# HGRN level scores in two batches of four levels, with the far half as a step of its own

## The chip, the cores and the metric

The kernel runs on one core of a Trainium2 chip. Its time is the device time of one execution in microseconds (us), the median over several runs. A core has five engines that run side by side, each through its own list of instructions in order: TensorE (PE, matrix products; PEld are its weight loads), VectorE (DVE), ScalarE (ACT), GpSimd (POOL) and SyncE (SP). They wait for one another through semaphores. SP and POOL issue the transfers (DMA) between DRAM and the on-chip memory.

## The reference, cut to what matters

One transformer-like layer over 256 latent tokens and 256 context tokens, width 2048, all in float32. The part around the change is the token mixer's gated linear recurrence (HGRN2) in both directions, with 8 heads of 128 channels:

```python
def step(s, xs):
    qc, kc, vc, gc = xs
    a = jnp.cumsum(gc, axis=2)
    inter = jnp.einsum('bhtk,bhkv->bhtv', qc * jnp.exp(a), s)
    diff = a[:, :, :, None, :] - a[:, :, None, :, :]
    decay = jnp.exp(jnp.where(tri[:, :, None], diff, -jnp.inf))
    scores = jnp.einsum('bhtk,bhsk,bhtsk->bhts', qc, kc, decay)
    intra = jnp.einsum('bhts,bhsv->bhtv', scores, vc)
    s_new = exp(a_last) * s + einsum('bhsk,bhsv->bhkv', kc * exp(a_last - a), vc)
    return s_new, inter + intra

def hgrn_bidir(q, v, gf, gb, s0f, s0b):
    o_f, s_f = hgrn_chunk_scan(q, gf[1], v, gf[0], s0f)
    o_b, s_b = hgrn_chunk_scan(fl(q), fl(gb[1]), fl(v), fl(gb[0]), s0b)
    return o_f + fl(o_b), s_f, s_b
```

Each output token reads each earlier token (in the other direction each later one) with a score that is a product over channels of query, key and all forget gates between the two. The remaining layer is large matrix products: an input projection of 2048 x 11264, two branch projections, an output projection, and an MLP of 2048 x 8192 and back.

## The kernel before, in words

TensorE's large products use a split form: each float32 weight tile of 128 x 1024 is loaded as `raw`, copied by ScalarE to its high half `whi` (L124), and VectorE makes the low half `wlo` (L127). Four such pairs are kept ready ahead of their use (`AHEAD = 4`). Lines 188, 255 and 257 are the products with them; L188 runs as two matmuls with `whi` and one with `wlo` per 128 rows of weights. Between the tiles stand products of vectors with the modulation weights on VectorE (L1314).

The heads are generators (`head`, L1419). While TensorE works through the input projection, `pump` (L161) is called after every few large matmuls and gives some microseconds of credit, and up to three generators emit their next instructions: a positive `yield` uses credit, `yield None` ends the generator's turn until the next call. For the heads, a call comes after 12 L188 matmuls, and later after 8 of L255 and 8 of L257. A scheduler then sets the order on each engine from this; on TensorE it keeps the order in which the program emits, but for one piece. Each engine runs its list as it stands and waits where something is not ready.

A head does this. It holds in `x6` six blocks of 256 columns, with queries and keys of both directions (128 channels by 256 tokens). For a level m, tokens that lie in neighbouring blocks of m score each other; after each level `decay(m)` (L1461) multiplies the gates into one half of each pair of blocks, so the next level can work on blocks twice as wide. The levels are 0 (the token itself), 1, 2, 4, 8, 16, 32, 64 and 128. For levels up to 64, ScalarE gathers the two sides of the product, `left` and `right` (`side`, L1455, the copies are at L1458), four matmuls of 64 output columns by 64 (L1497) write the scores of the 256 tokens into a PSUM bank, and masked copies on VectorE (L1514) put each level's scores into its places of `sc`. The bank holds several levels, and they are multiplied in one batch. The last level of a batch reads its right side straight from `x6` through `halves`, so that its decay must wait until the batch has read it. Level 128, called far, is two matmuls of 128 columns read in place (L1504). Where a batch stands between large products, TensorE goes from weights of 128 columns to two halves of 64 columns and back.

After level 128 the keys are needed with tokens on partitions: VectorE flips 32 x 32 squares (L1523), POOL writes the page to DRAM as `kthere` (L1526) and reads it back in four pieces (L1528), ScalarE copies it as `kt` (L1534), and TensorE builds the states (L1540). ScalarE copies them (L1543), and the head's output is the product of the queries with the states (L1549) and of the scores with the values (L1551). A head waits in its first steps until the head two before it has ended; `x6` has two buffers.

Of the kernel before, what the change touches and what calls it, by code (L numbers as in the profile page):

```python
# [15 lines left out]
P = 128  # L16
T = 256
# [120 lines left out]
class Kernel:  # L138
# [1280 lines left out]
    def head(self, h, e, vp):  # L1419
# [8 lines left out]
        nc = self.nc  # L1428
# [8 lines left out]
        x6 = self.sp.tile([P, 6 * T], F32, name="x6", tag="x6", bufs=2)  # L1437
# [8 lines left out]
        sc = self.small(512, "sc")  # L1446
        sc4 = sc.rearrange("p (c t) -> p c t", c=4)
        near = sc[:, P:2 * P]
        near2 = near.rearrange("p (b t) -> p b t", b=2)

        def halves(o, step, n, m):

            return bass.AP(x6.tensor, x6.offset + o, [x6.ap[0], [2 * m, n // (2 * m)], [step + m, 2], [1, m]])

        def side(name, o, step, m):  # L1455

            t = self.small(T, name)
            nc.scalar.copy(out=t.rearrange("p (n s m) -> p n s m", s=2, m=m), in_=halves(o, step, T, m))  # L1458
            return t

        def decay(m):  # L1461

            lo = x6[:, 0:3 * T].rearrange("p (n w) -> p n w", w=2 * m)[:, :, 0:m]
            hi = x6[:, 3 * T:6 * T].rearrange("p (n w) -> p n w", w=2 * m)[:, :, m:2 * m]
            d = e[:, 0:4 * T].rearrange("p (n w) -> p n w", w=2 * m)
            nb = 3 * T // (2 * m)
            no = T // (2 * m)
            nc.vector.tensor_tensor(lo, lo, d[:, 0:nb, m:m + 1].broadcast_to([P, nb, m]), op=ALU.mult)
            nc.vector.tensor_tensor(hi, hi, d[:, no:no + nb, 0:1].broadcast_to([P, nb, m]), op=ALU.mult)
            if m < 128:  # L1470
                nc.vector.tensor_tensor(d[:, :, 0:1], d[:, :, 0:1], d[:, :, m:m + 1], op=ALU.mult)

        for levels in ((0, 1, 2), (4, 8, 16), (32, 64, 128)):
            ops = []
            for m in levels:
                if m == 0:
                    ops.append((m, ks, q))
                    continue
                if m == 128:
                    yield None  # L1480
                    break
                left = side("left", T, 3 * T, m)
                right = None
                if m != levels[-1]:
                    right = side("right", 2 * T, T, m)
                ops.append((m, left, right))
                yield None
                if right is not None:
                    decay(m)
                    yield 1.2  # L1490
            ps = self.bank()
            for n, (m, left, right) in enumerate(ops):
                for b in range(2):
                    for g in range(2):
                        o = b * P + g * 64
                        r = b * P + (1 - g) * 64 if m == 64 else o
                        nc.tensor.matmul(ps[64 * g:64 * g + 64, n * P + b * 64:n * P + b * 64 + 64], left[:, o:o + 64],  # L1497
                                         right[:, r:r + 64] if right is not None else halves(2 * T + o, T, 64, m), start=True, stop=True)
            if levels[-1] == 128:
                far = self.bank()  # L1500
                for b in range(2):
                    w = x6[:, T:T + P] if b == 0 else x6[:, 4 * T + P:5 * T]
                    r = x6[:, 3 * T + P:4 * T] if b == 0 else x6[:, 2 * T:2 * T + P]
                    nc.tensor.matmul(far[:, b * P:(b + 1) * P], w, r, start=True, stop=True)  # L1504
            for n, (m, _, _) in enumerate(ops):
                pv = ps[:, n * P:(n + 1) * P].rearrange("p (b t) -> p b t", b=2)
                if m == 0:
                    nc.scalar.copy(out=near, in_=ps[:, n * P:(n + 1) * P])
                elif m == 64:
                    for g in range(2):  # L1510
                        nc.scalar.copy(out=sc4[64 * g:64 * g + 64, 0::3, 64 - 64 * g:128 - 64 * g], in_=pv[64 * g:64 * g + 64])
                else:
                    i = LEVELS.index(m)
                    nc.vector.copy_predicated(near2, self.masks[:, i:i + 1, :].broadcast_to([P, 2, 64]), pv)  # L1514
            if levels[-1] == 128:
                for g in range(2):
                    nc.scalar.copy(out=sc4[64 * g:64 * g + 64, 0::3, 64 * g:64 * g + 64], in_=near2[64 * g:64 * g + 64])
                nc.scalar.copy(out=sc4[:, 1:3, :], in_=far[:, :T].rearrange("p (b t) -> p b t", b=2))
            decay(levels[-1])
            yield 1.8  # L1520
        flip, back = e[:, 0:512], e[:, 512:1024]
        for d, o in enumerate((0, 5 * T)):
            nc.vector.transpose(out=flip.rearrange("p (j b r) -> p b j r", j=4, b=4)[:, 2 * d:2 * d + 2],  # L1523
                                in_=x6[:, o:o + T].rearrange("p (b j r) -> p b j r", b=2, j=4))
# [12 lines left out]
        ps = self.bank()  # L1537
# [8 lines left out]
        for tb in range(2):  # L1546
            o = po[:, tb * P:(tb + 1) * P]
# [6 lines left out]
        o = self.at(self.on, h)  # L1554
# [182 lines left out]
```

## Time and profile before

| what | value |
|---|---|
| median of 3 runs | 1623.03 us (1620.81 to 1623.83) |
| the profiled execution | 1622.89 us, span 1620.8 us |
| TensorE busy | 1603.9 us, 99% |
| VectorE busy | 1160.9 us, 72% |
| ScalarE busy | 803.8 us, 50% |
| GpSimd busy | 74.0 us, 5% |
| mean granted TensorE clock | 0.999 |
| moved by DMA | 395.21 MB, 244 GB/s |

The profile is of one execution. The span runs from its first to its last instruction; the time has 2.1 us around it. A row of a timeline has the start in us from the span's start, the length in us, the engine, the line of the kernel, the operation, the tile it writes and those it reads, and in brackets the idle time ahead of it and what ended that. An x behind it counts records; an fp32 matmul with fp32 operands leaves two records. Matmuls overlap, so the time that one costs is read from start to start and not from its length. In a row of grouped instructions the figures behind the bar are busy us, mean ns of one, and the idle time ahead of them.

### The profile page before, as it was taken

The page shows a single profiled execution, that of the slowest core. Times are in us where ns is not written, and L with a number is a line of the kernel's source. Part 1 is how long each engine was busy: PE and PEld are TensorE (multiplying, and loading weights), DVE is VectorE, ACT ScalarE, POOL GpSimd, SP SyncE. Part 2 cuts the span into 40 slices and gives each one's busy share as a digit, 9 for nine tenths or more (in the row PEclk, how much of TensorE's full clock was granted, in tenths as well). Part 3 has the DMA queues.
Part 4 walks back from the last instruction along what each step waited for, and adds up shares of the span by engine and source line. Part 5 has one row for each costly group of instructions (what it writes and reads, how often), then busy time and mean ns, then how long its engine had stood idle before and what let it go on. Part 6 is the DMA issues. An engine that isn't in the chain of part 4 may idle for free.

```text
span 1620.8 us, 22095 instructions
## 1 busy us (share of the span) xinstructions
PE 1603.9 (99%) x8163; PEld 1321.3 (82%) x8163; DVE 1160.9 (72%) x1694; ACT 803.8 (50%) x1166; POOL 74.0 (5%) x138
## 2 busy tenths in 40 slices
PE   7999999999999999999999999999999999999998
PEld 5668888888888888888888888888888888888887
DVE  5786888888778889967887766555665656656556
ACT  6553445465554444653446655444443454435543
POOL 0000001001100000000000001000010011001000
PEclk9999999999999999999999999999999999999999
DMA  9997955554666566778887378866997688777663
GB/s 368 403 391 261 324 200 180 170 162 165 224 228 222 182 195 208 228 265 305 326 289 263 134 262 249 276 207 222 289 288 235 212 264 270 236 241 243 230 218 116
DMA packets 110813, 395.21 MB, mean 244 GB/s; under 512 B 13552, under 2 KB 14448, under 8 KB 110704
## 3 DMA queue, kind: packets, MB, share of 16 engines
q1 hardware_dynamic: 102096, 368.34, 66.4%
q0 software_dynamic: 8320, 25.19, 5.3%
q8 instruction: 64, 1.05, 0.3%
q14 instruction: 45, 0.37, 0.1%
q10 hardware_dynamic: 288, 0.26, 0.0%
HBM read 381.15 MB, written 12.58 MB: 243 GB/s over the span
## 4 chain that ended last, share of the span: by engine, by line
PE 94%; DMA 2%; DVE 2%; ACT 1%; issue 1%; SPq 0%; ACTq 0%; DVEq 0%
PE bank L188 83%; PE bank L255 5%; PE bank L257 2%; PE bank L1497 1%; DMA raw<-wi 1%; DVE wlo L127 1%; DMA x<-x 0%; DMA raw<-wpw 0%; PE bank L1549 0%; PE bank L1551 0%; ACT whi L124 0%; PE bank L1540 0%; DMA fg<-kthere 0%; PE bank L1504 0%; PE bank L1360 0%
## 5 line engine op out<-in xcount | busy, mean ns | idle before, releaser
L127 DVE TENSOR_TENSOR wlo<-raw,whi 128x1024 fp32r<-128x1024 f32 x488 | 593.1, 1223 | 328.5 <-ACT whi L124 324.6
L124 ACT ACTIVATE whi<-raw 128x1024 fp32r<-128x1024 f32 x488 | 512.2, 1058 | 577.2 <-PE bank L188 376.3
L188 PE MATMUL bank<-whi,h 128*128 128x512 f32 x2160 | 674.0, 390 | 2.0 <-DVE h L673 1.2
L188 PEld LDWEIGHTS bank<-whi,h 128*128 128x128 f32 x2160 | 405.2, 188 | 87.6 <-DVE h L673 2.0
L188 PE MATMUL bank<-wlo,h 128*128 128x512 f32 x1080 | 420.8, 390 | 1.4 <-DVE wlo L127 1.4
L188 PEld LDWEIGHTS bank<-wlo,h 128*128 128x128 f32 x1080 | 202.8, 188 | 44.7 <-DVE wlo L127 3.2
L188 PE MATMUL bank<-whi,hidh 128*128 128x512 f32 x503 | 195.0, 388 | 0.0
L188 PE MATMUL bank<-wlo,hidh 128*128 128x512 f32 x503 | 195.0, 388 | 0.0
L188 PE MATMUL bank<-whi,hidl 128*128 128x512 f32 x503 | 195.0, 388 | 0.0
L188 PE MATMUL bank<-h,whi 128*128 128x512 f32 x512 | 163.7, 401 | 0.3 <-DVE h L673 0.3
L188 PEld LDWEIGHTS bank<-h,whi 128*128 128x128 f32 x512 | 92.5, 188 | 23.9 <-issue 5.8
L188 PEld LDWEIGHTS bank<-whi,hidh 128*128 128x128 f32 x503 | 94.5, 188 | 19.5
L188 PEld LDWEIGHTS bank<-wlo,hidh 128*128 128x128 f32 x503 | 94.5, 188 | 19.3
L188 PEld LDWEIGHTS bank<-whi,hidl 128*128 128x128 f32 x503 | 94.5, 188 | 19.2
L188 PE MATMUL bank<-h,wlo 128*128 128x512 f32 x256 | 100.1, 391 | 0.0
L255 PE MATMUL bank<-h,whi 128*128 128x512 f32 x384 | 97.0, 394 | 0.0
L255 PEld LDWEIGHTS bank<-h,whi 128*128 128x128 f32 x384 | 69.1, 189 | 12.7
L1301 DVE SCALAR_TENSOR_TENSOR gacc<-raw,silu_c,gacc 128x1024 f32<-128x1024 f32 x60 | 76.7, 1278 | 0.0
L1314 DVE SCALAR_TENSOR_TENSOR raw<-raw,silu_row 128x1024 f32<-128x1024 f32 x64 | 76.6, 1218 | 0.0
L188 PEld LDWEIGHTS bank<-h,wlo 128*128 128x128 f32 x256 | 48.0, 188 | 10.0
L257 PEld LDWEIGHTS bank<-h,wlo 128*128 128x128 f32 x384 | 52.4, 190 | 3.8
L257 PE MATMUL bank<-h,wlo 128*128 128x256 f32 x384 | 53.5, 282 | 0.0
(252 smaller groups left out, 1377.0 us busy)
## 6 DMA issues: line engine op xcount, KB each, us to landing
raw<-w SPq DMA_DIRECT2D x256, 512.0 KB, 4.8
raw<-wi SPq DMA_DIRECT2D x172, 512.0 KB, 4.4
raw<-wmt SPq DMA_DIRECT2D x64, 512.0 KB, 4.1
raw<-wm SPq DMA_DIRECT2D x64, 512.0 KB, 4.7
rawpage<-wm SPq DMA_DIRECT2D x42, 512.0 KB, 10.0
raw<-wo SPq DMA_DIRECT2D x32, 512.0 KB, 4.6
raw<-who SPq DMA_DIRECT2D x16, 512.0 KB, 4.8
raw<-wpw SPq DMA_DIRECT2D x16, 512.0 KB, 5.5
```

Source lines behind the costliest of these rows:

```text
L124: kn.his.append(nc.scalar.activation(out=hi, in_=raw, func=AF.Copy))
L127: kn.los.append(nc.vector.tensor_tensor(lo, raw, hi.bitcast(F32), op=ALU.subtract))
L188: ins = fn(*args, **kw)
L255: nc.tensor.matmul(bank, w[0][:, cut(i)], x(k)[2], start=(k == 0), stop=False)
L257: nc.tensor.matmul(bank[:, T:], w[1][:, cut(i)], x(k)[0], start=False, stop=(k == nk - 1))
L1301: nc.vector.scalar_tensor_tensor(acc, raw, s, acc, op0=ALU.mult, op1=ALU.add)
L1314: nc.vector.scalar_tensor_tensor(raw, raw, 1.0, self.srow, op0=ALU.mult, op1=ALU.mult, accum_out=self.dot[:, 32 * j + b:32 * j + b + 1])
L1497: nc.tensor.matmul(ps[64 * g:64 * g + 64, n * P + b * 64:n * P + b * 64 + 64], left[:, o:o + 64], right[:, r:r + 64] if right is not None ...
```

## The change

The levels are computed in two batches, (0, 1, 2, 4) and (8, 16, 32, 64), where there were three, (0, 1, 2), (4, 8, 16) and (32, 64, 128). Level 64's two sides are read in place from `x6`; before, ScalarE gathered them. The first gathered right side of a batch is put into the second half of `sc`, not into a small buffer. The copies of the near scores into their final places follow the level-64 copies. The far half becomes a step of its own behind a turn's end (`yield None`), with its own decay and yields.

```diff
-        def side(name, o, step, m):
-
-            t = self.small(T, name)
+        def side(name, o, step, m, t=None):
+
+            t = self.small(T, name) if t is None else t
...
-        for levels in ((0, 1, 2), (4, 8, 16), (32, 64, 128)):
+        for levels in ((0, 1, 2, 4), (8, 16, 32, 64)):
             ops = []
             for m in levels:
                 if m == 0:
                     ops.append((m, ks, q))
-                    continue
-                if m == 128:
+                elif m == 64:
+                    ops.append((m, None, None))
+                else:
+                    left = side("left", T, 3 * T, m)
+                    right = side("right", 2 * T, T, m, sc[:, T:] if m == max(levels[0], 1) else None) if m != levels[-1] else None
+                    ops.append((m, left, right))
                     yield None
-                    break
-                left = side("left", T, 3 * T, m)
-                right = None
-                if m != levels[-1]:
-                    right = side("right", 2 * T, T, m)
-                ops.append((m, left, right))
-                yield None
-                if right is not None:
-                    decay(m)
-                    yield 1.2
+                    if right is not None:
+                        decay(m)
+                        yield 1.2
+            yield None
             ps = self.bank()
             for n, (m, left, right) in enumerate(ops):
                 for b in range(2):
                     for g in range(2):
                         o = b * P + g * 64
...
+                        if m == 64:
+                            w, r = x6[:, T + o + 3 * T * g:][:, :64], x6[:, 2 * T + b * P + (1 - g) * (T + 64):][:, :64]
+                        else:
+                            w, r = left[:, o:o + 64], right[:, o:o + 64] if right is not None else halves(2 * T + o, T, 64, m)
+                        nc.tensor.matmul(ps[64 * g:64 * g + 64, n * P + b * 64:n * P + b * 64 + 64], w, r, start=True, stop=True)
...
                     for g in range(2):
                         nc.scalar.copy(out=sc4[64 * g:64 * g + 64, 0::3, 64 - 64 * g:128 - 64 * g], in_=pv[64 * g:64 * g + 64])
+                        nc.scalar.copy(out=sc4[64 * g:64 * g + 64, 0::3, 64 * g:64 * g + 64], in_=near2[64 * g:64 * g + 64])
...
             decay(levels[-1])
-            yield 1.8
+            yield 1.9
+        yield None
+        far = self.bank()
+        for b in range(2):
+            w = x6[:, T:T + P] if b == 0 else x6[:, 4 * T + P:5 * T]
+            r = x6[:, 3 * T + P:4 * T] if b == 0 else x6[:, 2 * T:2 * T + P]
+            nc.tensor.matmul(far[:, b * P:(b + 1) * P], w, r, start=True, stop=True)
+        nc.scalar.copy(out=sc4[:, 1:3, :], in_=far[:, :T].rearrange("p (b t) -> p b t", b=2))
+        decay(128)
+        yield 1.2
```

The new lines are L1498 (the products, before L1497), L1509 (masked copies, before L1514), L1505 and L1506 (the copies of level 64 and of the near scores), L1517 (far, before L1504) and L1518 (its copy).

What moves on the engines is shown at three places. First TensorE at head 0 and the start of head 1, before; the rows left out are large products (L188), and `x_2161` and `x_2431` are the `x6` of heads 0 and 1:

```order
L1497 MATMUL bank<-q_1730,ksum 64x64 x4
L1497 MATMUL bank<-right,left 64x64 x4
L1497 MATMUL bank<-x_2161,left 64x64 x4
...
L1497 MATMUL bank<-right,left 64x64 x8
L1497 MATMUL bank<-x_2161,left 64x64 x4
...
L1497 MATMUL bank<-right,left 64x64 x8
L1504 MATMUL bank<-x_2161 128x128 x2
...
L1497 MATMUL bank<-q_1730,ksum 64x64 x4
L1497 MATMUL bank<-right,left 64x64 x4
...
L1497 MATMUL bank<-x_2431,left 64x64 x4
...
L1540 MATMUL bank<-v_1430,kt 128x128 x4
```

And with the change (head 1's `x6` is `x_2438`):

```order
L1498 MATMUL bank<-q_1730,ksum 64x64 x4
L1498 MATMUL bank<-sc,left 64x64 x4
L1498 MATMUL bank<-right,left 64x64 x4
L1498 MATMUL bank<-x_2161,left 64x64 x4
...
L1498 MATMUL bank<-sc,left 64x64 x4
L1498 MATMUL bank<-right,left 64x64 x8
L1498 MATMUL bank<-x_2161 64x64 x4
...
L1517 MATMUL bank<-x_2161 128x128 x2
...
L1540 MATMUL bank<-v_1430,kt 128x128 x4
L1498 MATMUL bank<-q_1730,ksum 64x64 x4
```

Three batches became two. From far to L1540 stand 60 large matmuls before and now; but head 1's first batch stood between them, and now stands behind L1540. Between the second batch and far stand 12 large matmuls.

Second, TensorE from head 4's far to its L1540 with the change (`x_3208` and `x_3495` are the `x6` of heads 4 and 5); the rows left out ahead of the batch are 36 matmuls of L188, those behind it 12. Before, 60 stood there in all, and a batch of three levels:

```order
L1517 MATMUL bank<-x_3208 128x128 x2
...
L1498 MATMUL bank<-q_1731,ksum 64x64 x4
L1498 MATMUL bank<-sc,left 64x64 x4
L1498 MATMUL bank<-right,left 64x64 x4
L1498 MATMUL bank<-x_3495,left 64x64 x4
...
L1540 MATMUL bank<-v_466,kt 128x128 x4
```

For head 7 the same stretch holds 48 matmuls of L255 and 48 of L257 before, and 40 and 40 with the change. In the other heads it holds what it held or more, but for head 6 (48 and 48 where there were 56 and 56, and a batch in both).

Third, VectorE at the end of head 7's levels with the change (`x_4126` is its `x6`):

```order
L1509 COPY_PREDICATED sc<-masks,bank 128x128
L1468 TENSOR_TENSOR x_4126<-x_4126,fg 128x6x64
L1509 COPY_PREDICATED sc<-masks,bank 128x128
L1469 TENSOR_TENSOR x_4126<-x_4126,fg 128x6x64
L1471 TENSOR_TENSOR fg<-fg 128x8
L127 TENSOR_TENSOR wlo<-raw,whi 128x1024 x2
L1468 TENSOR_TENSOR x_4126<-x_4126,fg 128x3x128
L1469 TENSOR_TENSOR x_4126<-x_4126,fg 128x3x128
L1314 SCALAR_TENSOR_TENSOR raw,dot<-raw,silu_row 128x1024
L1523 STREAM_TRANSPOSE fg<-x_4126 128x2x4x32 x2
```

Before, the flip followed the two decays of level 128 at once; now an L1314 stands between. At head 4 the flip follows the decays at once. At head 0, between the second batch's masked copies and the two decays of level 128 stand an L1471, an L1432 and two L1314, and an L1441 between these decays and the flip. From the last head on, the order of every engine is the same as before.

More of the change, by code (lines that the diff above doesn't have):

```diff
@@ L1495, in head @@
                         o = b * P + g * 64
[L1496 to L1504, printed above, removed]
+                        if m == 64:
[3 more added lines that the diff above has]
+                        nc.tensor.matmul(ps[64 * g:64 * g + 64, n * P + b * 64:n * P + b * 64 + 64], w, r, start=True, stop=True)
             for n, (m, _, _) in enumerate(ops):
```

4 lines of the change are left out of this document (removed).

## The prediction

> **What bounds the kernel now.** I read the page first (busy shares, then the chain that ended last), then the waits of TensorE over the stage of the heads, then TensorE's rows there.
>
> ```profile
> PE 1603.9 (99%) x8163; PEld 1321.3 (82%) x8163; DVE 1160.9 (72%) x1694; ACT 803.8 (50%) x1166; POOL 74.0 (5%) x138
> ...
> PE 94%; DMA 2%; DVE 2%; ACT 1%; issue 1%; SPq 0%; ACTq 0%; DVEq 0%
> ```
>
> TensorE is the chain: 94% of it. The heads run from 205 to 480 us. In that window the view of TensorE's waits has one row, and its timeline shows the place:
>
> ```profile
> PE bank L1549 <- ACT state L1543: 0.3, 1, 0.3
> ...
> 446.99 0.87 PE L257 MATMUL bank<-h,wlo 128*128 128x256 f32 x6
> 448.12 0.71 PE L1549 MATMUL bank<-state,x 128*128 128x128 f32 x4 [0.26 <-ACT state L1543]
> ```
>
> L257 matmuls start every 0.12 us, so the sixth started at 447.59 and the next start was due at 447.71; it came at 448.12. That 0.4 us is all that TensorE loses to others there. So an edit in the heads pays only if it shortens TensorE's own work, and costs only if TensorE is made to wait.
>
> **What a batch costs TensorE.** Timeline of TensorE around head 0's first batch, then around the four products of L1540 (an fp32 matmul is recorded twice, so x8 is four matmuls):
>
> ```profile
> 218.85 0.39 PE L188 MATMUL bank<-h,wlo 128*128 128x512 f32 x1
> 219.17 0.45 PE L1497 MATMUL bank<-q,ksum 128*64 128x64 f32 x8
> 219.45 0.40 PE L1497 MATMUL bank<-right,left 128*64 128x64 f32 x8
> 219.69 0.41 PE L1497 MATMUL bank<-x,left 128*64 128x64 f32 x8
> 220.03 0.73 PE L188 MATMUL bank<-h,whi 128*128 128x512 f32 x2
> 220.60 0.40 PE L188 MATMUL bank<-h,wlo 128*128 128x512 f32 x1
> 220.83 0.62 PE L188 MATMUL bank<-h,whi 128*128 128x512 f32 x2
> ...
> 221.53 0.62 PE L188 MATMUL bank<-h,whi 128*128 128x512 f32 x2
> ...
> 222.21 0.62 PE L188 MATMUL bank<-h,whi 128*128 128x512 f32 x2
> ```
>
> ```profile
> 253.68 0.39 PE L188 MATMUL bank<-h,wlo 128*128 128x512 f32 x1
> 253.91 1.05 PE L1540 MATMUL bank<-v,kt 128*128 128x128 f32 x8
> ...
> 255.49 0.61 PE L188 MATMUL bank<-h,whi 128*128 128x512 f32 x2
> ```
>
> Undisturbed, three L188 matmuls take 0.68 us (221.53 to 222.21), 0.227 each. From 218.85 to 220.83 are 1.98 us, of which four L188 starts (one wlo, two whi, one wlo) are 0.91; the batch cost 1.07. A level, once running, takes 0.24 (219.45 to 219.69); three are 0.70 to 0.72. What is left, **0.36 us, is paid once per batch**, at its two ends: going from 128-column weights to the 64-column halves and back. The L1540 group, with 128 columns, shows none of it: 253.68 to 255.49 is 1.81, less four L188 starts 0.90, for eight records of 0.113.
>
> **The change, part by part.**
>
> Batches. Before, the 64-column products stand in three batches a head, and head 1's first is cut in two by the order: 25. In the change's order they stand in two a head, head 1's second cut in two: 17. The number of matmuls is the same (32 of 64 columns and two of L1504, now L1517, a head). Eight ends saved are 8 x 0.36 = **2.9 us gained**. The far products now stand alone; with 128 columns they pay no switch, four records of 0.113 = 0.45, as they did inside the third batch.
>
> Copies. The sides are 11 copies a head instead of 12, 0.41 us each on ScalarE:
>
> ```profile
> L1458 ACT COPY left<-x 128x256 f32<-128x256 f32 x56 | 23.8, 425 | 45.9 <-DVE x L1469 43.2 <-DVE x L1441 2.3
> ```
>
> ScalarE is half idle and TensorE waits for it once; worth nothing. The decays, masked copies and the four copies of level 64 stay in number. A decay that must wait until the batch has read x6 in place is there three times a head as before (levels 2, 16, 128; now 4, 64, 128); behind it on VectorE stand the next halves of the weights, L127, of which four tiles are kept ready (AHEAD), 5.4 us of L188 each, so that wait is covered; with the cover gone each would cost what L127 comes too late. On ScalarE the two copies of the near scores (L1506) now stand between those of level 64 (L1505) and wait for the last masked copy, some 1.5 us behind the batch; the high halves of the weights (L124) queue behind them and have the same four tiles of cover.
>
> The late wait of head 6 (0.4 us above): in the change's order that state copy has 2 us more room, as its products come 18.4 us after far; I take the 0.4 as **gained**, with none as the other end.
>
> What gets shorter is the time left for the trip of the flipped keys. After far, VectorE decays level 128 and flips (L1523), POOL sends the page to DRAM (L1526) and fetches it back (L1528), ScalarE copies (L1534), TensorE needs it in L1540. Rows of heads 0, 1, 4 and 7, POOL and ScalarE, and TensorE's far and L1540:
>
> ```profile
> 242.92 0.69 POOL L1526 DMA_DIRECT2D kthere<-fg  x1 [242.48 <-DVE fg L1523]
> ...
> 274.41 0.56 POOL L1526 DMA_DIRECT2D kthere<-fg  x1 [24.35 <-DVE fg L1523]
> ...
> 365.84 0.56 POOL L1526 DMA_DIRECT2D kthere<-fg  x1 [20.85 <-DVE fg L1523]
> ...
> 463.74 0.56 POOL L1526 DMA_DIRECT2D kthere<-fg  x1 [27.00 <-DVE fg L1523]
> ```
>
> ```profile
> 252.19 0.62 ACT L1534 COPY kt<-fg 128x512 f32<-128x512 f32 x1 [0.58 <-DMA fg<-kthere]
> ...
> 283.06 0.62 ACT L1534 COPY kt<-fg 128x512 f32<-128x512 f32 x1 [0.67 <-issue]
> ...
> 375.29 0.62 ACT L1534 COPY kt<-fg 128x512 f32<-128x512 f32 x1
> ...
> 475.60 0.62 ACT L1534 COPY kt<-fg 128x512 f32<-128x512 f32 x1 [5.95 <-DMA fg<-kthere]
> ```
>
> ```profile
> 238.27 0.71 PE L1504 MATMUL bank<-x 128*128 128x128 f32 x4
> ...
> 477.46 0.39 PE L1540 MATMUL bank<-v,kt 128*128 128x128 f32 x2
> ```
>
> The trip, L1526 to L1534, is 9.3, 8.65, 9.45 and 11.9 us. Head 0 had 15.6 us from far (238.27) to L1540 (253.91), its copy done at 252.81: 1.1 us spare. Head 7's copy ended at 476.22, 1.2 us ahead of 477.46. TensorE does not skip a product that isn't ready, so its place in the order decides. In the change's order, from far to L1540:
> - head 0: 60 L188 matmuls, 13.6 + 0.45 = 14.05 us (before 15.6: head 1's first batch now stands behind L1540, not ahead of it);
> - head 4: 48 of them and a batch of four levels, 10.9 + 1.3 + 0.45 = 12.65 (12 matmuls fewer than before);
> - head 7: 40 of L255 and 40 of L257 (before 48 and 48), by the chain's rows below 5 x 2.79 + 0.45 = 14.4.
>
> ```profile
> 453.06 0.95 PE bank L257 x8
> 454.01 1.84 PE bank L255 x8
> ```
>
> The other heads have 15.4 us or more. And from far to L1526, by VectorE's rows of head 0 and the groups of the stage:
>
> ```profile
> 230.10 0.30 DVE L1514 COPY_PREDICATED sc<-masks,bank 128x128 f32<-128x128 uint8 x1
> ...
> 231.64 0.22 DVE L1471 TENSOR_TENSOR fg<-fg 128x32 f32<-128x32 f32 x1
> ...
> 239.76 0.55 DVE L1468 TENSOR_TENSOR x<-x,fg 128x384 f32<-128x384 f32 x1
> ...
> 240.70 1.22 DVE L1314 SCALAR_TENSOR_TENSOR raw<-raw,silu_row 128x1024 f32<-128x1024 f32 x1
> ...
> 241.84 0.77 DVE L1523 STREAM_TRANSPOSE fg<-x 128x256 f32<-128x256 f32 x2
> ...
> L1432 DVE TENSOR_SCALAR fg<-fg,lbm,lb 128x512 f32<-128x512 f32 x16 | 8.5, 539 | 0.0
> ...
> L1441 DVE TENSOR_TENSOR x<-fg,q 128x512 f32<-128x512 f32 x8 | 5.5, 686 | 0.0
> ```
>
> Masked copies with their decay are 1.55 (230.10 to 231.64), two decays 0.94, an L1314 1.14, a flip 0.77; POOL starts 0.3 behind it.
> - Head 0: VectorE starts as its second batch ends and does, in the change's order, 1.55 + 0.2 (L1471) + 0.5 (L1432) + 2 x 1.14 + 0.94 + 0.65 (L1441) + 0.77 = 6.9; far starts 2.8 after the batch (12 matmuls), so L1526 is at far + 4.4. With its trip of 9.3 and 0.70 for the copy and the way to TensorE: 14.4, **0.35 late**.
> - Head 4: far stands 24 matmuls behind the batch, VectorE is done by then; far's end 0.7, 0.94, 0.77, 0.3: L1526 at far + 2.7; with 9.45 and 0.70: 12.9, **0.25 late**.
> - Head 7: the same with one L1314 between, far + 3.9; with 11.9 and 0.70: 16.5, **2.05 late**.
>
> Sum of the lateness: 2.65 us. With the shortest trip, 8.65, all three are on time (13.75, 12.1, 13.25): 0. With 11.9 at all three: 2.95 + 2.65 + 2.05 = 7.65. These are the ends; I take each head's own trip, since head 7's stage is where the last two heads' tiles stream faster, one per 2.79 us instead of 5.4.
>
> **Sum**, against the profiled execution's 1622.89 (its span 1620.8 and 2.1 around it): -2.9 - 0.4 + 2.65 = -0.65 us. Its time is 0.14 under the median 1623.03, and the same difference is applied there: **1622.4 us**. Beyond the heads the orders of all engines are the same, and nothing is costed.
>
> **Rivals.**
> 1. *The keys are never late and the gain arrives whole.* For it: the trip can be 8.65, and 8.65 suffices at all three heads. Against it: in head 7's own stage the trip took 11.9, and only 9.8 would do there. Time 1623.03 - 3.3 = 1619.7. [...]
>
> ```profile
> kthere<-fg POOLq DMA_DIRECT2D x8, 256.0 KB, 3.5
> fg<-kthere POOLq DMA_DIRECT2D x32, 64.0 KB, 3.6
> ```
>
> 2. *Slower: the trip of the keys is 11.9 us also in the L188 stage* (the place: L1528 to L1534 of heads 0 and 4, while weight tiles stream). Price: the 7.65 above, 1623.03 - 3.3 + 7.65 = 1627.4, and about 1 us more at each head with 15.4 us of room. It decides from a summed lateness of 3.3 us on. Against it: the three trips of that stage quoted here are 8.65 to 9.45.
> 3. *The change does not save what it says*: the 0.36 belongs to something else in the batch and grows with its levels. Then -0.4 + 2.65 = +2.3, 1625.3. Against it: the L1540 group, which shows none.
>
> **How the numbers follow.** Forecast 0.62, its own range 1621.2 to 1624.2 (lateness of 1.5 to 4.5 us); rival 1 0.28; rival 2 0.07; rival 3 0.03. About 0.2%, 3.2 us, is what a measurement of this kernel can tell from none: its runs shown spread over 3.0. Rival 1 lies just on that bound (1619.8), half of it counts as faster: 0.14. Slower is rival 2 and 0.01 from the others: 0.08. The rest, 0.78, is the same. The range leaves out the lower part of rival 1 and all of rival 2: 1619.5 to 1625.2.
>
> **What would show it.** On TensorE: 17 groups of 64-column products and 1.3 us for one of four levels; if it is 1.6, rival 3. Far to L1540 at heads 0, 4 and 7 longer than 14.05, 12.65 and 14.4, with a wait of L1540 for L1534 in the view of waits, longest at head 7; without these waits, rival 1. The trips between L1526 and L1534 tell rival 2. Waits of the first products of a batch for their side copies, or of L188 for L127, would prove the cover wrong, and the prediction with it.

## The result, and the profile after

The changed kernel takes 1630.85 us (median of 6 runs, 1629.79 to 1631.77) against 1622.26 us of the kernel before beside it (6 runs, 1620.81 to 1623.83): ratio 1.0053, 95% interval 1.0040 to 1.0065. It is slower by 8.6 us. Forecast were 1622.4 us and a range up to 1625.2; the slower rival stood at 1627.4 with a chance of 0.07. The profiled execution of the changed kernel took 1630.1 us, its span is 1628.3 us.

The page's chain of work, after:

```profile
PE 83%; issue 6%; DMA 5%; DVE 3%; ACT 1%; POOL 1%; SPq 0%; ACTq 0%; POOLq 0%; DVEq 0%
```

TensorE was 94% of the chain before; now 83%, with DMA and "issue" in its place. The view of TensorE's waits from 205 to 500 us, the heads, says which. Before it had one row of 0.3 us there; now the one row is another:

```profile
PE bank L1540 <- ACT kt L1534: 9.2, 5, 3.5
```

L1540, the products with the flipped keys, waits five times for the copy of these keys. The timeline of TensorE names the heads (0, 3, 4, 5 and 7; heads 1, 2 and 6 are on time):

```profile
253.98 1.16 PE L1540 MATMUL bank<-v,kt 128*128 128x128 f32 x8 [1.43 <-ACT kt L1534]
...
350.98 1.16 PE L1540 MATMUL bank<-v,kt 128*128 128x128 f32 x8 [1.19 <-ACT kt L1534]
382.59 1.16 PE L1540 MATMUL bank<-v,kt 128*128 128x128 f32 x8 [1.04 <-ACT kt L1534]
418.24 1.16 PE L1540 MATMUL bank<-v,kt 128*128 128x128 f32 x8 [2.06 <-ACT kt L1534]
...
493.56 1.16 PE L1540 MATMUL bank<-v,kt 128*128 128x128 f32 x8 [3.47 <-ACT kt L1534]
```

The brackets sum to 9.2. Counted from start to start each is some 0.16 more (head 0: the matmul ahead started at 252.16, the next start was due 0.227 later, it came at 253.98, so 1.59), 10.0 in all.

**The gain came too.** A batch of four levels on TensorE's timeline, after:

```profile
284.47 0.39 PE L188 MATMUL bank<-h,wlo 128*128 128x512 f32 x1
284.79 0.45 PE L1498 MATMUL bank<-q,ksum 128*64 128x64 f32 x8
285.07 0.40 PE L1498 MATMUL bank<-sc,left 128*64 128x64 f32 x8
285.30 0.40 PE L1498 MATMUL bank<-right,left 128*64 128x64 f32 x8
285.54 0.40 PE L1498 MATMUL bank<-x,left 128*64 128x64 f32 x8
285.87 0.73 PE L188 MATMUL bank<-h,whi 128*128 128x512 f32 x2
286.43 0.40 PE L188 MATMUL bank<-h,wlo 128*128 128x512 f32 x1
286.67 0.62 PE L188 MATMUL bank<-h,whi 128*128 128x512 f32 x2
```

From 284.47 to 286.67 are 2.20 us, less four L188 starts 0.91: 1.29, the 1.3 of the prediction, against 1.07 for three levels.

**A second cost behind the longest wait.** TensorE's timeline and its windows around head 7's wait (columns of a window: length, busy time of PE, PEld, DVE, ACT, POOL, the granted clock, the DMA share, GB/s):

```profile
494.48 3.37 PE L255 MATMUL bank<-h,whi 128*128 128x512 f32 x8
497.65 1.43 PE L257 MATMUL bank<-h,wlo 128*128 128x256 f32 x8
```

```profile
480.00:489.00 9.00, 9.00 (x53) 7.88 (x52) 7.40 (x11) 3.45 (x4) 2.74 (x5) 1.00 0.89 279
489.80:493.50 3.70, 0.29 (x3) 0.09 (x1) 0.05 (x2) 0.61 (x2) 0.00 (x0) 1.00 1.01 327
...
495.00:497.70 2.70, 2.70 (x8) 2.03 (x7) 1.06 (x2) 0.40 (x2) 0.00 (x0) 0.50 0.36 94
```

After 3.7 us without matmuls the granted clock is 0.50 from 494.92 to 498.34, 3.4 us (the last row lies inside this stretch): six steps of L255 take 0.427 us instead of 0.227 and some of L257 0.213 instead of 0.12, 1.6 us lost in a stretch where nothing waits.

Against the profiled execution of before, whose span is 7.5 us shorter, the terms are: waits of L1540 +10.0, the slow clock +1.6, far of head 3 behind a decay +0.3, a late L127 near 790 us +1.0, the batches -3.0 (measured apart below), head 6's state copy -0.4, and the start of the program, where a wait for the load of x was 0.9 us instead of 2.9 so that TensorE stands 2.4 us earlier at 205 us, -2.4. That is +7.1 of 7.5. The start differs from execution to execution (a second profile of the changed kernel has 2.8 us in that wait); the rest belongs to the change, but for the 1.0 at 790 us, which is there in one profile of the best kernel below and not in the other.

### The profile page after: what moved, and what is told of

The parts are those of the page before. It is cut to its first block, busy times and chain, and to the rows that moved or that the text cites. A ratio compares the mean times of both kernels' runs of the same rounds, so it can differ in the third digit from the quotient of the medians.

```text
span 1628.3 us, 22077 instructions
## 1 busy us (share of the span) xinstructions
PE 1603.5 (98%) x8163; PEld 1320.2 (81%) x8163; DVE 1159.1 (71%) x1694; ACT 799.8 (49%) x1158; POOL 74.5 (5%) x138
## 4 chain that ended last, share of the span: by engine, by line
PE 83%; issue 6%; DMA 5%; DVE 3%; ACT 1%; POOL 1%; SPq 0%; ACTq 0%; POOLq 0%; DVEq 0%
PE bank L188 78%; PE bank L255 3%; PE bank L257 1%; DMA fg<-kthere 1%; DMA raw<-wi 1%; DMA kthere<-fg 1%; DVE wlo L127 1%; POOL fg L1528 1%; DMA rawpage<-wms 1%; DMA x<-ctx 1%; DMA raw<-wpw 1%; ACT whi L124 0%; PE bank L1498 0%; DVE raw L1314 0%; PE bank L1540 0%
## 5 line engine op out<-in xcount | busy, mean ns | idle before, releaser
L127 DVE TENSOR_TENSOR wlo<-raw,whi 128x1024 fp32r<-128x1024 f32 x488 | 593.0, 1221 | 326.6 <-ACT whi L124 324.9
L188 PE MATMUL bank<-whi,h 128*128 128x512 f32 x2160 | 674.2, 390 | 2.3 <-DVE h L673 1.2
L188 PEld LDWEIGHTS bank<-whi,h 128*128 128x128 f32 x2160 | 405.2, 188 | 88.3 <-DVE h L673 2.0
L188 PE MATMUL bank<-wlo,h 128*128 128x512 f32 x1080 | 420.9, 390 | 1.7 <-DVE wlo L127 1.7
L188 PEld LDWEIGHTS bank<-wlo,h 128*128 128x128 f32 x1080 | 202.8, 188 | 45.1 <-DVE wlo L127 3.4
L188 PE MATMUL bank<-whi,hidh 128*128 128x512 f32 x503 | 195.0, 388 | 0.0
L188 PE MATMUL bank<-wlo,hidh 128*128 128x512 f32 x503 | 195.0, 388 | 0.0
L188 PE MATMUL bank<-whi,hidl 128*128 128x512 f32 x503 | 195.0, 388 | 0.0
L188 PE MATMUL bank<-h,whi 128*128 128x512 f32 x512 | 163.9, 401 | 0.2 <-DVE h L673 0.2
L188 PEld LDWEIGHTS bank<-h,whi 128*128 128x128 f32 x512 | 92.3, 188 | 23.5 <-issue 5.8
L188 PEld LDWEIGHTS bank<-whi,hidl 128*128 128x128 f32 x503 | 94.4, 188 | 19.5
L188 PEld LDWEIGHTS bank<-wlo,hidh 128*128 128x128 f32 x503 | 94.4, 188 | 19.5
L188 PEld LDWEIGHTS bank<-whi,hidh 128*128 128x128 f32 x503 | 94.4, 188 | 19.1
L188 PE MATMUL bank<-h,wlo 128*128 128x512 f32 x256 | 100.0, 391 | 0.0
L255 PE MATMUL bank<-h,whi 128*128 128x512 f32 x384 | 98.6, 399 | 0.0
L255 PEld LDWEIGHTS bank<-h,whi 128*128 128x128 f32 x384 | 69.7, 191 | 13.0
L1314 DVE SCALAR_TENSOR_TENSOR raw<-raw,silu_row 128x1024 f32<-128x1024 f32 x64 | 76.6, 1218 | 0.9 <-DMA raw<-wmt 0.9
L188 PEld LDWEIGHTS bank<-h,wlo 128*128 128x128 f32 x256 | 48.1, 188 | 10.0
L257 PEld LDWEIGHTS bank<-h,wlo 128*128 128x128 f32 x384 | 52.8, 192 | 3.9
L257 PE MATMUL bank<-h,wlo 128*128 128x256 f32 x384 | 53.8, 283 | 0.0
## 6 DMA issues: line engine op xcount, KB each, us to landing
rawpage<-wm SPq DMA_DIRECT2D x42, 512.0 KB, 10.2
```

The source lines that it names most:

```text
L127: kn.los.append(nc.vector.tensor_tensor(lo, raw, hi.bitcast(F32), op=ALU.subtract))
L188: ins = fn(*args, **kw)
L255: nc.tensor.matmul(bank, w[0][:, cut(i)], x(k)[2], start=(k == 0), stop=False)
L257: nc.tensor.matmul(bank[:, T:], w[1][:, cut(i)], x(k)[0], start=False, stop=(k == nk - 1))
L1314: nc.vector.scalar_tensor_tensor(raw, raw, 1.0, self.srow, op0=ALU.mult, op1=ALU.mult, accum_out=self.dot[:, 32 * j + b:32 * j + b + 1])
```

## The experiments

My theory: the batches of four save what was predicted, and the whole loss is that L1540 stands in TensorE's order ahead of the moment at which the keys are back from DRAM. The rivals: the batches of four or the far step cost time themselves; the trip is slow for a reason of its own; the length of a trip is chance.

### L1540 one step later

```diff
-        for _ in range(3):
+        for _ in range(4):
             yield None
         kt = self.small(512, "kt")
```

> The changed kernel with one more step before the copy of the keys (four instead of three), so that L1540 stands one group of matmuls further on: 71 or 72 L188 between far and L1540 at heads 0 to 4 instead of 48 or 60. Theory (the keys come too late for L1540, the batches themselves save what was predicted): room of 17.2 to 18.5 us against 13.9 to 18.0 us that the heads used in the changed kernel, so only head 7 can still wait, 0.8 us; 1630.85 less the 10.0 us of waits, less 1.2 of slow matmuls behind head 7's wait, less 1.0 of the wait at 792 us, plus 0.8 = 1619.5, between 1618.5 and 1621.5. Rival (batches of four or the far step of its own cost time on TensorE or make something else late): the place of L1540 does not matter, at most 2 us below the changed kernel, so above 1628.5.

Measured: 1620.07 us, ratio 0.9990 (0.9981 to 0.9999), no wait of L1540 at any head. So the place of L1540 is what costs. Two new rows stand in TensorE's timeline, 1.5 us together:

```profile
416.83 0.71 PE L1549 MATMUL bank<-state,x 128*128 128x128 f32 x4 [1.04 <-ACT state L1543]
...
454.03 0.71 PE L1549 MATMUL bank<-state,x 128*128 128x128 f32 x4 [0.50 <-ACT state L1543]
```

### No trip at all, with two batches and with three

In both kernels, the changed one and the one before:

```diff
-        flip, back = e[:, 0:512], e[:, 512:1024]
+        flip = back = e[:, 0:512]
...
-        there = self.dr.tile([P, 512], F32, name="kthere", tag="kthere", bufs=2)
-        nc.gpsimd.dma_start(there, flip)
-        for j in range(4):
-            nc.gpsimd.dma_start(back[32 * j:32 * j + 32]...
```

> The changed kernel without the trip of the keys through DRAM: L1534 copies straight from the flipped page, so the state is computed from keys in the wrong order of partitions; the amount of work of TensorE, VectorE and ScalarE stays. Theory: no wait of L1540; the pure worth of two batches, 1622.3 - 2.9 - 0.4 = 1619.0, between 1618 and 1620.5. Rival (batches of four or the far step cost time): stays above 1626.

> The kernel before without the trip, left out in the same way. Theory: its keys were never late, so the trip costs it nothing: within 0.7 us of 1622.3, and 2.5 to 3.7 us above two_batches_no_trip. Rival (batches of four cost time): below two_batches_no_trip.

Measured on one chip, beside 1621.86 for the kernel before: two batches 1618.70 (ratio 0.9978, 0.9969 to 0.9987), three batches 1621.73 (1.0000, 0.9991 to 1.0009). The difference is 3.03 us: this is what two batches are worth on their own, 2.9 predicted. In neither has TensorE any wait in the heads. Both copy the flipped page directly, so the keys stand in the wrong order in both, and TensorE, VectorE and ScalarE keep their work. And the trip cost the kernel before nothing: its keys were always in time.

### Four batches, no trip

```diff
-        for levels in ((0, 1, 2, 4), (8, 16, 32, 64)):
+        for levels in ((0, 1), (2, 4), (8, 16), (32, 64)):
```

> two_batches_no_trip with the eight levels in four batches of two, (0,1), (2,4), (8,16), (32,64); the trip is left out as there. 34 groups of 64-column products in the order of TensorE instead of 17. Theory (0.36 us per group, paid at its two ends): 17 x 0.36 = 6.1 us more than two_batches_no_trip, 1624.8, between 1623.8 and 1626.5. Rival (the cost belongs to the levels, not to the group): within 1 us of 1618.7.

Measured: 1627.34 us, 8.6 above the two batches, more than the 6.1 expected and 0.8 above the range. (The two were measured on different chips; the kernel before beside them differs by 0.2, and the two profiled executions are 8.0 apart.) A batch of two levels in its timeline:

```profile
341.00 0.39 PE L188 MATMUL bank<-h,wlo 128*128 128x512 f32 x1
341.32 0.45 PE L1498 MATMUL bank<-sc,left 128*64 128x64 f32 x8
341.60 0.40 PE L1498 MATMUL bank<-x,left 128*64 128x64 f32 x8
341.93 0.73 PE L188 MATMUL bank<-h,whi 128*128 128x512 f32 x2
342.50 0.40 PE L188 MATMUL bank<-h,wlo 128*128 128x512 f32 x1
```

The next L188 starts at 342.73, so the batch costs 1.73 less 0.91 = 0.82; four levels cost 1.29. So a level costs 0.235 and the group 0.35, as predicted, and 17 groups are 5.9 of the 8.6. Two waits account for another 1.4: the readers of the state wait 0.5 once, and the readout at about 650 us waits 1.1 instead of 0.2 for its scaled rows. Some 1.3 us stay without a row.

### The kernel before, with L1540 one step earlier

```diff
-        for _ in range(3):
+        for _ in range(2):
             yield None
```

> The kernel before with one step fewer ahead of the copy of the keys (two instead of three): L1540 stands 12 L188 earlier, 48 of them between far and L1540, 12.4 us of room where the heads needed 13.9 to 16.1 us from far to the end of the keys' copy. Theory: waits of L1540 for L1534 of 1 to 2.5 us at nearly every head, 10 to 17 us in all, 1632 to 1640, with the batches left alone. Rival (the batches are what costs): within 2 us of 1622.3.

Measured: 1631.52 us, ratio 1.0061 (1.0048 to 1.0073), with three batches and far where it was. The view of waits has the changed kernel's row:

```profile
PE bank L1540 <- ACT kt L1534: 7.3, 6, 2.3
```

It is 9.7 us slower than the kernel before (1621.86 beside it), 0.5 short of the range that was expected; the waits are 7.3 us and not the 10 to 17 expected, as the trips of heads 4 and 5 took 7.7 and 8.4 us and these two heads were in time. One step, 2.7 us of TensorE's work at each head, makes the kernel before as slow as the changed one. Its trips left it little: in the kernel before the copies of the keys of heads 0 to 5 ended only 0.6 to 1.4 us ahead of L1540 (head 4's at 375.91, with L1540 at 376.47).

### The far step alone, with three batches

The changed kernel's code with its levels in three batches:

```diff
-        for levels in ((0, 1, 2, 4), (8, 16, 32, 64)):
+        for levels in ((0, 1, 2), (4, 8, 16), (32, 64)):
```

> The changed kernel's code with its levels in three batches, (0,1,2), (4,8,16), (32,64): the far half is a step of its own and level 64 is read in place as in the change, but the number of groups is 25 as before, so nothing of the 2.9 us is saved. From far to L1540 the order leaves 12.3, 13.9, 15.1, 11.9, 15.1, 21.0, 18.2 and 14.4 us at heads 0 to 7. Theory (the far step of its own is what makes the keys late; the batches of four are the gain): waits of L1540 at heads 0, 3 and 7, 1 to 3.6 us each, with up to 1 us at some other, 6 to 12 us with the slow matmuls behind head 7's wait; 1628 to 1634. Rival (the batches of four make the keys late): no wait, 1622.3 within 1 us.

Measured: 1634.54 us (4 runs, 1630.68 to 1636.71), ratio 1.0077 (1.0063 to 1.0091). Rows of its profile:

```profile
260.36 1.16 PE L1540 MATMUL bank<-v,kt 128*128 128x128 f32 x8 [2.46 <-ACT kt L1534]
...
474.60 0.60 PE L1549 MATMUL bank<-state,x 128*128 128x128 f32 x3 [2.98 <-ACT state L1543]
...
507.78 1.16 PE L1540 MATMUL bank<-v,kt 128*128 128x128 f32 x8 [0.90 <-ACT kt L1534]
```

So the loss does not need the batches of four. The waits fell on heads 0 and 7 as expected, but head 3 waited 0.2 us only, and head 6's late state copy, not expected, cost 3.0. Its median lies 0.5 above the range given; the profiled execution took 1630.7 at a granted clock of 0.998, the three others 1634.3 to 1636.7 at 0.996 and 0.997, so its rows show only part of the median's loss.

### A second profile of the changed kernel

> The changed kernel once more, unaltered, for a second profile of it. If the length of each head's trip belongs to the place in the program (what else streams at that moment), the waits of L1540 come back at heads 0, 3, 4, 5 and 7 and each trip from L1526 to L1534 within 0.5 us of 9.8, 9.1, 10.0, 11.3, 10.1, 13.5, 9.3, 12.8. If it is chance of one execution, the trips of single heads differ by over 1 us and the waits fall on other heads, with a sum still near 10 us.

Measured: 1633.62 us (one run). The trips from L1526 to L1534 are 7.1, 9.4, 10.4, 11.2, 9.6, 13.4, 10.0 and 13.5 us (first profile 9.8, 9.1, 10.0, 11.3, 10.1, 13.5, 9.3, 12.8). Seven of eight agree within 0.8 us: the length belongs mostly to the place in the program. Head 0 is the exception: 2.7 us less, and it does not wait; the other four wait again, 0.7 to 4.4 us. My bound of 0.5 us was too tight, and the execution has a part in it.

### Lighter weight tiles around heads 5 to 7

Windows over these trips say what the places share. Before, heads 3, 5, 6 and 7:

```profile
337.92:347.26 9.34, 9.34 (x62) 7.54 (x61) 7.60 (x16) 4.21 (x9) 2.73 (x5) 1.00 0.74 226
393.76:403.08 9.32, 9.32 (x62) 7.52 (x61) 6.42 (x14) 4.19 (x8) 2.73 (x5) 1.00 0.49 171
428.82:441.11 12.29, 12.29 (x91) 10.73 (x90) 8.17 (x13) 3.98 (x7) 4.14 (x7) 1.00 0.91 276
463.74:475.60 11.86, 11.86 (x69) 10.38 (x68) 6.25 (x9) 3.29 (x6) 2.74 (x5) 1.00 0.86 263
```

The changed kernel, the same heads:

```profile
339.04:350.31 11.27, 10.75 (x74) 8.43 (x72) 6.24 (x10) 1.95 (x3) 2.92 (x5) 1.00 0.72 225
404.12:417.57 13.45, 12.06 (x95) 10.40 (x93) 7.85 (x11) 3.45 (x4) 4.14 (x7) 1.00 0.93 304
443.30:452.59 9.29, 9.29 (x54) 8.13 (x53) 7.87 (x11) 4.60 (x7) 2.74 (x5) 1.00 0.86 287
480.14:492.89 12.75, 9.95 (x59) 8.65 (x57) 8.11 (x12) 3.45 (x4) 2.73 (x5) 1.00 0.93 290
```

Four of the five trips with a DMA share of 0.86 and more (the number before the last) take 11.9 to 13.5 us; head 6's in the changed kernel, 9.3, is the exception. Head 5 is the one that crossed over: its far came at 389.12 before and at 400.34 now, and its trip moved out of the L188 stage, which ends at 400 to 401 us, into the stage of L255 and L257. (Before, its keys had landed after 8.2 of the 9.3 us, and ScalarE came to the copy 1.1 us later, so the step up to 13.5 is larger still.)

Head 3 went from 9.3 to 11.3 us at nearly the same share, 0.74 and 0.72. What changed there is when SyncE issues weight tiles (`raw`). Its issues around this trip, before and then after (`wi` and `wmt` are weights in DRAM, SPq is SyncE's queue):

```profile
338.77 3.17 SPq L86 DMA_DIRECT2D raw<-wi  x2
348.15 1.93 SPq L86 DMA_DIRECT2D raw<-wmt  x2
```

```profile
345.20 1.93 SPq L86 DMA_DIRECT2D raw<-wmt  x2
347.94 0.33 SPq L86 DMA_DIRECT2D raw<-wi  x1
```

The read-back (L1528 to L1534) ran from 342.81 to 347.26 before, with no tile issued in it: 4.45 us. With the change it ran from 344.47 to 350.31, with three: 5.84 us. Over the 16 trips of these two profiles, the read-back took 4.30 to 4.45 us in the three where no tile was issued between 1 us ahead of its start and 4 us behind (heads 0, 3 and 4 before), and 5.4 to 8.5 us, 7.3 in the median, in the seven with three. This is a reading across trips; no experiment moved single tiles.

The experiment takes the load away in the stage of L255 and L257:

```diff
+            if self.done + len(self.raws) in self.half:
+                self.dma = kn.nc.sync.dma_start(raw[:, 0:512], ap[:, 0:512])
+            else:
                 self.dma = kn.nc.sync.dma_start(raw, ap)
```

> The changed kernel with the 32 weight tiles that L255 and L257 use (from 400 to 512 us) loaded by half: only the first 512 of their 1024 columns come from memory, and the high and low halves are made from these columns twice, so two column blocks are computed with the wrong weights; all engines keep their work, and the loads of that stretch shrink from 512 to 256 KB a tile. The trips of heads 5 to 7 run there; their windows showed a DMA share of 0.93, 0.86 and 0.93 and 13.5, 9.3 and 12.8 us. Theory (the length of a trip goes with what else the DMA engines carry): share 0.5 to 0.7, trips of 8 to 10 us, no wait of L1540 at heads 5 and 7, and 7 us less, 1623 to 1625; heads 0, 3 and 4 wait as before. Rival (the trip is long for a reason of its own, its place on POOL or its descriptors): trips of heads 5 and 7 still over 12 us, their waits stay.

Measured: 1621.82 us (one run). The trips of heads 5 to 7:

```profile
403.04:411.62 8.58, 8.58 (x69) 7.53 (x69) 7.04 (x11) 3.45 (x4) 4.13 (x7) 1.00 0.75 232
439.27:447.55 8.28, 8.28 (x50) 7.27 (x49) 7.04 (x10) 5.11 (x9) 2.73 (x5) 1.00 0.58 194
476.72:485.96 9.24, 9.24 (x55) 8.14 (x54) 7.64 (x11) 3.45 (x4) 2.73 (x5) 1.00 0.84 242
```

8.6, 8.3 and 9.2 us instead of 13.5, 9.3 and 12.8; no wait is left at heads 5 and 7. So what the weight tiles put on the DMA engines stretches the trip there. The share of a window does not say all of it: 0.84 goes with 9.2 us here (0.5 to 0.7 was expected at all three). Of the heads ahead of that stretch only head 3 still waits, 1.8 us; heads 0 and 4 were in time as well (head 0's trip was 7.5), so the time is below the 1623 to 1625 expected.

### One step more ahead of the readers of the state

The kernel with L1540 one step later, and:

```diff
         nc.scalar.copy(out=st, in_=ps[:, 0:T])
         yield None
+        yield None
```

> two_batches_later_products with one more step between the state copy L1543 and the products L1549 that read it. In two_batches_later_products no product of L1540 waits any more, but L1549 waits for the state copy at heads 5 and 6, 1.04 and 0.50 us, because ScalarE comes to that copy late. Theory: these 1.5 us go and nothing else is left: 1620.1 - 1.5 = 1618.6, the time of two_batches_no_trip (1618.7), between 1617.8 and 1619.6. Rival (the 1.4 us between the two kernels are the trip's load on the DMA engines, which slows the stream of weights elsewhere): stays at 1620.1.

Measured: 1624.67 us, ratio 1.0020 (1.0011 to 1.0029): 4.6 us slower instead of 1.5 faster. The waits of L1549 are gone, and the keys of head 6 are late:

```profile
462.19 1.53 PE L1540 MATMUL bank<-v,kt 128*128 128x128 f32 x8 [2.70 <-ACT kt L1534]
```

```profile
447.62:461.52 13.90, 11.87 (x94) 10.25 (x92) 9.90 (x15) 3.60 (x6) 2.74 (x5) 1.00 0.98 325
...
464.00:466.00 2.00, 2.00 (x6) 1.60 (x5) 2.00 (x7) 0.48 (x2) 0.00 (x0) 0.50 0.32 88
```

A head may begin only when the one two ahead of it has ended, so later readers push the later heads back: head 6's far is at 440.84 instead of 431.18. Its trip now ran at a DMA share of 0.98 and took 13.9 us, with the half clock behind the wait. Moving a step buys room for one wait and moves the later trips against the stream of tiles.

### The keys first

The other way to give the keys time is to start them earlier. The flip needs only the keys' part of level 128, which far does not read. So this part is decayed directly behind the second batch, then come flip and trip, then far, then the rest of the decay from a saved copy of its factors:

```diff
+        f = self.small(8, "far")
+        nc.vector.tensor_copy(f[:, 0:6], e[:, 128:896:128])
+        nc.vector.tensor_tensor(x6[:, 0:P], x6[:, 0:P], f[:, 0:1]..., op=ALU.mult)
+        nc.vector.tensor_tensor(x6[:, 5 * T + P:6 * T], x6[:, 5 * T + P:6 * T], f[:, 5:6]..., op=ALU.mult)
         flip, back = e[:, 0:512], e[:, 512:1024]
...
+        yield 1.6
         yield None
         far = self.bank()
...
-        decay(128)
+        for o, i in ((T, 2), (2 * T, 4), (3 * T + P, 1), (4 * T + P, 3)):
+            nc.vector.tensor_tensor(x6[:, o:o + P], x6[:, o:o + P], f[:, i:i + 1]..., op=ALU.mult)
         yield 1.2
...
-        yield 0.9
         for _ in range(3):
```

> The changed kernel with the keys' part of level 128 decayed, the flip and the trip put directly behind the second batch, ahead of the far step instead of behind it; the other parts of level 128 are decayed after far from a saved copy of their six factors (four more small operations on VectorE a head). From the second batch to L1540 are 18.4 to 23.1 us of TensorE's work. Theory: the trip starts some 4.5 us behind the batch instead of 7 to 9, and with trips of 9 to 13.5 us and 0.7 for the copy it needs 14.2 to 18.7 us, so no wait of L1540 of over 0.5 us: 1619 (1618 to 1621). Rival (the trip is slow because the weight tiles stream while it runs, and an earlier start only meets more of them: trips grow by what the start gains): waits stay, above 1626.

> two_batches_keys_first once more, unaltered, beside three_batches_keys_first and the kernel before on one chip: 1617.2 within 0.8 us, 4.4 us below the kernel before, no wait of L1540 in its profile.

Measured: 1617.22 us, ratio 0.9974 (0.9963 to 0.9984), and in another set of runs 1618.44, ratio 0.9975 (0.9966 to 0.9984): 4 us faster than the kernel before and 13 faster than the changed one. Both medians missed their ranges, the first 0.8 below its 1618 to 1621, the second 0.4 above its 1616.4 to 1618.0; against the kernel before beside each they are 4.4 and 3.9 us. Its lines are numbered anew: L1521 sends the page, L1531 is far, L1545 are the products. Head 5 on POOL and TensorE:

```profile
395.84 0.56 POOL L1521 DMA_DIRECT2D kthere<-fg  x1 [24.01 <-DVE fg L1518]
```

```profile
397.93 0.61 PE L1531 MATMUL bank<-x 128*128 128x128 f32 x4
413.62 1.06 PE L1545 MATMUL bank<-v,kt 128*128 128x128 f32 x8
```

The trip starts 2.1 us ahead of far instead of 3.8 behind it. It runs to 405.53, 9.7 us at a DMA share of 0.64 instead of 13.5 at 0.93, and there is no wait of the products at any head in either profile. The rival, that an earlier trip only meets more of the tiles, fell.

### The keys first, with three batches

```diff
-        for levels in ((0, 1, 2, 4), (8, 16, 32, 64)):
+        for levels in ((0, 1, 2), (4, 8, 16), (32, 64)):
```

> two_batches_keys_first with its levels in three batches, (0,1,2), (4,8,16), (32,64): the trip ahead of far, 25 groups of 64-column products instead of 16. From far to L1540 12.3 us and more, from the last batch 18.1 us and more, so no wait of L1540. Theory: 9 x 0.35 = 3.2 us more than two_batches_keys_first, 1620.4, between 1619.3 and 1621.8. Rival (the early trip is what gains over the kernel before, and the batches little): within 1 us of two_batches_keys_first.

Measured: 1622.65 us, ratio 1.0005 (0.9996 to 1.0013), 4.2 us above the kernel with two batches on the same chip. So the early trip alone gains nothing over the kernel before, whose keys were in time; the gain is the batches', and the early trip is what lets it through. The difference is 1.0 more than the 3.2 expected, the time 0.8 above its range, and the readout waits 1.5 us at about 650 us, where two batches have 0.2:

```profile
PE bank L1582 <- DVE o L1577: 1.5, 1, 1.5
```

## Why the prediction was wrong

- **What bounds the kernel** was read rightly: an edit in the heads pays by TensorE's own work and costs by TensorE's waits. Both happened.
- **Batches, -2.9**: right. 17 groups, 1.29 us for four levels, 3.03 us between the two kernels without a trip. Rival 3 is dead: what a batch costs beside its levels is 0.36 predicted, 0.35 in batches of two.
- **Copies, decays and masked copies at nothing**: right but for 0.3 us, by which far of head 3 was late. No first product of a batch and no L188 of this stretch waited for its input.
- **Head 6's state copy, -0.4**: right here; that wait is gone. It is not safe: L1549 waited for a state copy again, 0.3 to 3.0 us, in four of the kernels in which the steps moved.
- **The time left to the trip**: the rooms read from the order were right (14.05 us predicted at head 0; the second profile, where head 0 does not wait, shows 14.06 between far and L1540).
- **From far to L1526**: heads 4 and 7 were summed as 2.7 and 3.9 and measured 3.1 and 4.6; head 0 as 4.4 and measured 5.2. Each is 0.4 to 0.8 late, 1.85 us of the 10.0.
- **The trip**: this is the step that failed. "I take each head's own trip" supposed that a head keeps its trip when the order moves it. Head 5 did not: 9.3 us at a DMA share of 0.49 became 13.5 at 0.93, because its far came 11 us later; the faster tiles, counted for "the last two heads", met the last three. Head 3's went from 9.3 to 11.3 at the same share, with three tiles issued in its read-back instead of none. And "the other heads have 15.4 us or more" took the trips of before as enough to call these heads safe, though a room of 15.3 us had left the same heads only 0.6 to 1.4 us of slack. Heads 3 and 5, for which no lateness was counted, waited 1.35 and 2.2 us from start to start; heads 0, 4 and 7, counted with 0.35, 0.25 and 2.05, waited 1.6, 1.2 and 3.6. Of the 7.35 us above the 2.65 in the sum, the trips have some 5.5 and L1526 has 1.85. The profile before could have warned: head 2's trip, which the prediction did not quote, took 10.2 us in the L188 stage.
- **The slow clock** was in no term: 1.6 us. The last section shows that whether a wait of 2 to 3.5 us brings it goes in part by the execution.

Rival 2 had the direction and the mechanism (keys later than L1540, price per head, and more at the heads with 15.4 us), but a wrong place: it made the L188 stage's trips as long as head 7's. In truth they stayed at 9.1 to 11.3 there. That its 7.65 us came near the 10.0 is luck: it priced heads 0, 4 and 7 at 2.95, 2.65 and 2.05, and the waits were 1.6, 1.2 and 3.6 there and 3.6 more at heads 3 and 5. Rival 1 fell in the changed kernel, and it is what the kernel with the keys first became. The shortest trips of the kernel with L1540 one step later took 7.1 and 7.55 us at a DMA share of 0.55 and 0.64 (heads 1 and 0), but at 0.64 head 2's trip before took 10.2, and at 0.98 one took 13.9. So the runs show no one price of a trip beside a stream of tiles.

## What to carry to other kernels

A slack of 1 us on a transfer that takes 7 to 14 us is no slack: before an edit moves the reader or the start of such a transfer, the room is to be compared with the longest trip in the profile, and the trip is to be taken from the stretch into which it moves, by the DMA share there and by the tiles issued while it runs, not from the one it leaves. Where a change shortens TensorE's work and something off TensorE sets its next step, the latency has to be given back at its start: here the keys went ahead of the far products and the gain of the batches came through whole, while giving more room behind them moved the next heads into the heavier stream.

## What the hardware showed beyond that

Short waits of TensorE can cost more than themselves. Of ten gaps of 2.1 to 4.5 us from start to start of two matmuls in the heads of these profiles, six were followed by steps of 0.427 us instead of 0.227, with a granted clock of 0.50, and four were not; shorter gaps had none behind them. The length alone does not decide. The same gap at head 5 of the changed kernel, 2.34 us in the first profile, had no slow steps behind it, and in the second profile, 2.26 us, had six. A gap of 3.26 us, the state copy's wait in the kernel with the far step alone (471.34 to 474.60), had none.

The moments at which the clock changes lie whole steps of 3.413 us apart in three profiles. In the second of the changed kernel it falls at 419.17 us and rises at 422.58, one step later. In the first it falls at 494.92, 142 such steps behind the first record of the full clock at 10.23, and rises one step later. In the profile of before it falls at 1618.86, 470 steps behind the first record at 14.60. Here are the windows of these steps around the two gaps of head 5, in the second profile and then in the first (TensorE's busy time stands behind the window and its length):

```profile
415.75:419.17 3.42, 1.43 (x13) 1.23 (x12) 0.55 (x3) 1.15 (x4) 0.00 (x0) 1.00 0.52 178
419.17:422.58 3.41, 3.41 (x12) 2.73 (x11) 3.41 (x9) 2.36 (x5) 0.00 (x0) 0.50 0.02 5
```

```profile
416.42:419.83 3.41, 1.59 (x11) 1.50 (x12) 1.33 (x5) 1.93 (x5) 0.00 (x0) 1.00 0.38 139
```

The gap that was followed by the half clock left TensorE busy for 1.43 of 3.42 us, a share of 0.42; the other one 1.59 of 3.41, 0.47. In the first profile, the window ahead of the half clock at head 7, 491.51 to 494.92, has 1.36 of 3.41, 0.40; every other window of the heads at full clock has 0.47 or more, as the profile counts busy time. So a wait of much the same length had slow steps behind it in one execution of the kernel and none in the other; the steps of the two lie 0.66 us apart (419.17 and 419.83). Whether the share of a window is what decides, no run here tests.
